# Low parts of the feed-forwards' own weight pool: subtracted on GpSimd instead of VectorE

## The chip, the cores and the metric

The kernel runs on one core of a Trainium2 chip. The metric is the device time of one execution in microseconds (us). The engines named below are TensorE (PE for its matmuls, PEld for its weight loads), VectorE (DVE), ScalarE (ACT), GpSimd (POOL) and SyncE (SP), whose queue issues the DMAs.

## The reference

256 tokens of 1024 features go through two transformer blocks, all in float32. What matters here is the feed-forward, which occurs six times with its own weights each time (two in the first block, four in the second):

```python
def swiglu(x, w_gate, w_up, w_down):      # [256,1024] x [1024,2816], [1024,2816], [2816,1024]
    return (jax.nn.silu(x @ w_gate) * (x @ w_up)) @ w_down

x = layer_norm(alpha * x + 0.5 * swiglu(x, ...))         # first block, twice, a hybrid attention mixer between them
h = h + 0.5 * _swiglu(_rmsnorm(h, g), w_gate_up, w_down)  # second block, four times, with a short
                                                          # convolution, shared keys and values, sparse attention between
```

## The kernel before

All weights arrive as float32 and are split into two parts of a type that TensorE takes at full rate: the high part is the rounded word (a copy on ScalarE), the low part is the word less its high part (a subtraction on VectorE). Every product is then three matmuls: high by high, high by low, low by high (`mm3`, lines 122 to 126). Activations are split in the same way after they were transposed on TensorE (`to_xt`, lines 232 to 246).

The function `unit` (lines 98 to 111) brings in a unit of weights, 128 partitions x 1024 words: one DMA of 512 KB on SP's queue into a tile `raw`, of which there are five; then, for each half of 512 columns, the copy on line 108 and the subtraction on line 109. A raw tile is free for a later DMA when both halves are subtracted. The parts go to tiles `whi` and `wlo`. By default these come from the pool `main`, six of each in a ring. With `pool=fp` they come from the pool of the feed-forward that is running, with the tag "d" and `nd` tiles of each (six; four in the fifth feed-forward). Two places ask for that:

```python
hi, lo = unit(wd[f * P:f * P + P, :], 1, D, fp, nd, "d")                      # line 418, down weights
sides.append(list(units(w, 0, 512, 2, **(dict(pool=fp, bufs=nd, tag="d") if i else {}))))   # line 384, first up weights
```

The pool `fp` is opened at the start of each `ffn` and takes the memory of the one before, so its tiles can be written when the feed-forward before has done with them.

A feed-forward goes as follows. `first` (lines 351 to 391) computes the first 512 hidden features token tile by token tile (two tiles of 128 tokens): gate and up for tile 0, then, after the transposes of tile 1, gate and up for tile 1. Its gate weights (four units) come from `main`; its up weights (four units) from `fp`, except in the very first feed-forward, where both come from `main`. For tile 0 the two transposes of tile 1's activations stand ahead of the last two of the eight chunks of the up product (`xt.ahead(1)`, line 388). Then `block` (lines 393 to 412) does 256 hidden features at a time with the weights stationary, nine times: gate (two units), up (two units), then the down product of the features before (`down`, lines 416 to 423: one unit for 128 features). The last six rows of down weights (four in the fifth) are kept and used at the end half by half, so that the residual, the norm and the transposes for what follows (`done`) can start while TensorE still works.

Between stages stands a chain through several engines: the residual add and the statistics on VectorE and ScalarE, the inverse root on GpSimd (`rsqrt`, line 230: a power on a column of 128 x 1), the scaling by the gains on VectorE (lines 278, 279, 303), the transposes on TensorE (line 238), their split by ScalarE and VectorE (lines 240, 241).

The order of the instructions on each engine's queue is set before the run by a planner that follows the program's order as priorities and its own estimate of when data and tiles are there; each engine then works its queue strictly in order and waits at its head. Only the instructions of the very first gate weights are kept in the program's order (`order=tc.keep_in_program_order`).

The five feed-forwards with first up weights in `fp` are called F2 to F6 below, in order of time. F2 follows the mixer's output projection, F3 follows F2 directly, F4 follows the convolution, F5 the shared keys and values, F6 the sparse attention's output projection.

Of the kernel before, what the change touches and what calls it, by code (L numbers as in the profile page):

```python
# [10 lines left out]
F32 = mybir.dt.float32  # L11
# [3 lines left out]
OP = mybir.AluOpType  # L15
# [19 lines left out]
def bcast_rows(ap, n, parts=P):  # L35
    """A DRAM vector of n elements, read into every partition."""
    return bass.AP(tensor=ap.tensor, offset=ap.offset, ap=[[0, parts], [1, n]])


class Turned(list):  # L40
    """Split transposes of activations; `need` brings in those of a tile of tokens, `ahead` a part of them."""

# [19 lines left out]
def weave(steps, others, rate):  # L62
    """After each of `steps`, `rate` of `others`."""
    due = 0.0
    for _ in steps:
        due += rate
        while due >= 1:
            next(others, None)
            due -= 1
# [3 lines left out]
def hybrid_blocks(  # L73
# [6 lines left out]
    nc = tc.nc  # L80
# [15 lines left out]

    # ---- weights: float32 words split into two float32r parts whose sum is exact
    def unit(src, nk, n, pool=None, bufs=6, tag="", order=lambda i: i):
        """src: DRAM [nk * 128, n] -> (high, low), each [128, nk, n]."""
        w = nk * n  # L100
        pool = pool or main
        raw = main.tile([P, UNIT], F32, tag="raw", name="raw", bufs=5)
        hi = pool.tile([P, UNIT], F32R, tag=f"whi{tag}", name="whi", bufs=bufs)
        lo = pool.tile([P, UNIT], F32R, tag=f"wlo{tag}", name="wlo", bufs=bufs)
        nc.sync.dma_start(raw[:, :w].rearrange("p (k n) -> p k n", k=nk),
                          src.rearrange("(k p) n -> p k n", p=P))
        for c in (slice(0, w // 2), slice(w // 2, w)):
            order(nc.scalar.activation(hi[:, c], raw[:, c], AF.Copy))  # L108
            order(nc.vector.tensor_tensor(lo[:, c], raw[:, c], hi[:, c].bitcast(F32), op=OP.subtract))  # L109
        return (hi[:, :w].rearrange("p (k n) -> p k n", k=nk),  # L110
                lo[:, :w].rearrange("p (k n) -> p k n", k=nk))

    def units(src, n0, n, per, **kw):
        """Columns n0:n0+n of src [K, N], `per` chunks of 128 rows at a time."""
        nk = src.shape[0] // P
        for k0 in range(0, nk, per):
            c = min(per, nk - k0)
# [4 lines left out]
    def mm3(ps, s, m, start, stop, **kw):  # L122
        """ps (+)= s.T @ m for split operands; what is dropped is the product of the low parts."""
        nc.tensor.matmul(ps, lhsT=s[0], rhs=m[0], start=start, stop=False, **kw)  # L124
# [3 lines left out]
    def projecting(xt, src, n0, n, done, per=2, lead=0, ws=None):  # L128
        """done(t, ps): ps[:, :n] = tokens of tile t @ src[:, n0:n0+n]; in steps. The first `lead` chunks go
        through one tile of tokens before they go through the other."""  # L130
        nk = src.shape[0] // P
# [35 lines left out]
    def projecting_t(xt, src, n0, nm, done, per=2):  # L167
        """done(m, ps): ps [128 features, 256 tokens] of feature tile m, from the column n0 on; in steps."""
        nk = src.shape[0] // P
# [21 lines left out]
    def projecting_wide(xt, src, done, nxt=None, at=1, tail=4, bank=None, k0=0):  # L191
        """done(t, h, ps): half h of tokens @ src [K, 1024]; the last rows tile by tile and half by half; in
        steps. nxt: what `done` goes on to turn."""
        nk = src.shape[0] // P
# [27 lines left out]

    # ---- constants
    ident = const.tile([P, P], F32)
# [7 lines left out]
    def to_xt(src, t, xt, nk=KD, k1=0, then=None):  # L232
        """Token-major src [128, nk * 128] -> split transposes in xt[:][:, k1:k1+nk, tile t]."""
        def turn(k0):
# [51 lines left out]
    def rms_stat(t, i):  # L286
        """Sum of the squares of half i; with the second one, the factors of the tile."""
        if i == 0:
# [42 lines left out]

    # ---- feed-forward
    def ffn(xt, wg, wu, wd, done, nxt=None, at=1, nd=6, tail=6, hook=None, ws=None):
        """Hidden features in blocks: the first token by token, so that it starts with one tile of
        tokens; the others with the weights stationary. Each block goes on into the down product."""
        with tc.tile_pool(name="ffn", bufs=1) as fp:
# [106 lines left out]

    # ======== first block
    xt = new_xt()
    ws = units(ffn_w_gate[0, 0], 0, 512, 1, order=tc.keep_in_program_order)
    head = []
# [18 lines left out]
    def later(**aps):  # L466
        """Gains that are read in the middle of the feed-forward."""
        def load(f0):
# [6 lines left out]

    # ---- mixer
    xt2 = new_xt()
    with tc.tile_pool(name="mix", bufs=1) as mp:
        win = w_in[0]
        def qkv(i, first, got):  # L480
            """Queries and keys [384 features, 256 tokens], values [tokens, 6, 64 and a one]."""
            c0 = 1152 * i
# [27 lines left out]
        def scores(qh, kh, slope, sums=None):  # L510
            """exp of the biased scores less their maximum; columns 0:128 for tile 0, the rest tile 1."""
            ps = tpb("s")
# [19 lines left out]
        def values(pt, ops, j, v, hh, w):  # L532
            """ops[:, t, j] = the turned weights of tile t @ v."""
            for b, t, kt in ((0, 0, 0), (1, 1, 0), (2, 1, 1)):
# [12 lines left out]
        def heads(weigh, v, w, end):  # L547
            """weigh(hh) gives the weights of a head; end(ops, h0) takes three heads @ values. In steps,
            each head's products one head behind its scores."""
            s, ops = {}, None  # L550
# [22 lines left out]
        def attend_diff(o, q, k, v):  # L573
            """Weights less lambda times the other ones, both over the sum of the first ones; the latter
            is divided by at the end."""
            r0 = mp.tile([P, NT, 6], F32, name="r0")
# [29 lines left out]
        def attend_sb(o, q, k, v):  # L606
            """Keys on partitions: columns 0:256 are keys of tile 0 with all queries, 256:384 keys of
            tile 1 with queries of tile 1. Two heads at a time, in steps."""
            nb = 2
# [55 lines left out]
        def gates(i, gt):  # L665
            """sigmoid(x) = (tanh(x / 2) + 1) / 2, of branch i."""
            for hf in range(2):
# [89 lines left out]
        def attend(i, steps, rest, rate):  # L757
            """The attention of branch i, with `rest` between its steps; its result is turned later."""
            o = o_tile()
# [25 lines left out]

    # ---- second feed-forward, into the second block
    xt1 = new_xt()
# [11 lines left out]

    # ======== second block  # L800
    def gate_up(l, i):
# [6 lines left out]

    # ---- short convolution, feature-major
    yt = new_xt()  # L810
# [65 lines left out]

    # ---- shared keys and values
    kv_stack = ctx.enter_context(ExitStack())
# [51 lines left out]

    # ---- compressed keys and values: blocks of 32 tokens as 16 chunks of two tokens
    posr = cmpp.tile([36, P], F32, name="posr")
# [7 lines left out]
    fs = new_xt()  # L940
    # for keys and for values: of 16 chunks the high parts of 64 blocks, then their low parts
    fs = [x.rearrange("p a b -> p (a b)").rearrange("p (j e n) -> p j e n", j=16, e=2) for x in fs]
# [93 lines left out]

    # ---- sparse attention: with 256 tokens all four blocks are selected and the window spans all
    with tc.tile_pool(name="nsa", bufs=1) as ap:
# [19 lines left out]

        # queries, high part on partitions 0:64 and low part on 64:128, head by head
        qs = new_xt()  # L1060
# [60 lines left out]

        # keys: window tile 1, window tile 0, compressed, selection tile 0, selection tile 1
        ks = tuple(ap.tile([P, 4, 528], F32R, name=f"ks{i}") for i in range(2))
        nc.scalar.activation(ks[0], kraw, AF.Copy)
        nc.vector.tensor_tensor(ks[1], kraw, ks[0].bitcast(F32), op=OP.subtract)

        # gates: high and low parts of their 48 columns of weights side by side
        graw = main.tile([P, UNIT], F32, tag="raw", name="graw", bufs=5)[:, 0:KD * 48].rearrange("p (k n) -> p k n", n=48)
# [20 lines left out]

        # compressed values, one diagonal block for each of 8 heads  # L1150
        vcb = ap.tile([P, 2, 8, HD], F32, name="vcb")
# [17 lines left out]
        def score(hh):  # L1169
            """Scores of one head against all its keys, and their exponentials."""  # L1170
            hf, hq, g = hh // 8, hh % 8, hh // 4
# [20 lines left out]
        def turn(hh):  # L1192
            """Keys onto partitions."""
            for b, s in enumerate(state[hh]):
# [25 lines left out]
        def compressed(hf):  # L1220
            """Weights of the compressed keys for eight heads, then their share of the output."""
            p3 = pc[hf].rearrange("p t h n -> p (t h) n")
# [117 lines left out]
```

## Time and profile before

| | |
|---|---|
| median of 3 runs | 1636.39 us (1635.88 to 1636.52) |
| span of the profiled execution | 1633.7 us |
| TensorE matmuls busy | 1617.4 us, 99% |
| TensorE weight loads busy | 1469.7 us, 90% |
| VectorE busy | 1035.8 us, 63% |
| ScalarE busy | 843.9 us, 52% |
| GpSimd busy | 51.1 us, 3% |
| 16 DMA engines | 56.9% on the weights' queue |
| TensorE's granted clock | full in all slices |

The profile gives no other time of the profiled execution than its span, from the first instruction to the last; the medians of the runs lie 2.7 us above it. Busy shares are means over stages. A wait is idle time of an engine and the event that ended it. Lines are those of the code before the change.

### The profile page before, as it was taken

How to read it: one execution, taken by the hardware profiler on the slowest of the kernel's cores; microseconds unless marked ns; L12 is line 12 of the kernel's file. 1: busy time of each engine (PE TensorE's matmuls, PEld its weight loads, DVE VectorE, ACT ScalarE, POOL GpSimd, SP SyncE). 2: the span in 40 equal slices, each digit the busy share in tenths (PEclk: the TensorE clock that was granted, in tenths of full speed). 3: DMA queues.
4: the chain of work that ended last, by engine and by line, in shares of the span. 5: the costliest groups of instructions: out<-in, count | busy, mean ns of one | idle time of the engine just before them, and what ended most of it. 6: DMA issues, size and time to landing. Idle time of an engine off the chain costs nothing.

```text
span 1633.7 us, 27122 instructions
## 1 busy us (share of the span) xinstructions
PE 1617.4 (99%) x10487; PEld 1469.7 (90%) x10487; DVE 1035.8 (63%) x2038; ACT 843.9 (52%) x1628; POOL 51.1 (3%) x101
## 2 busy tenths in 40 slices
PE   8999999999999999999999999999999999999999
PEld 7999899888799998999899899988899988889998
DVE  6655567768865458555566755557676568775552
ACT  6544266664564445444354644436546448664441
POOL 1000000000000000000000000001000012100000
PEclk9999999999999999999999999999999999999999
DMA  9756354555585666655455765646648522175550
GB/s 318 241 181 197 112 164 127 175 169 176 175 265 180 193 193 207 193 181 194 131 180 167 250 189 181 202 139 206 196 146 290 182 85 89 53 229 183 183 191 27
DMA packets 190222, 291.74 MB, mean 179 GB/s; under 512 B 11088, under 2 KB 135308, under 8 KB 190092
## 3 DMA queue, kind: packets, MB, share of 16 engines
q1 hardware_dynamic: 190092, 290.00, 56.9%
q8 instruction: 82, 1.34, 0.4%
q14 instruction: 48, 0.39, 0.1%
HBM read 288.91 MB, written 1.05 MB: 177 GB/s over the span
## 4 chain that ended last, share of the span: by engine, by line
PE 95%; DVE 2%; ACT 1%; DMA 1%; issue 1%; POOL 0%; SPq 0%; ACTq 0%; POOLq 0%
PE acc L124 21%; PE acc L126 21%; PE acc L125 21%; PE tp L124 8%; PE tp L125 8%; PE tp L126 8%; PE tp L238 1%; PE ops L1207 1%; PE tp L1197 1%; DVE wlo L109 1%; DMA raw<-in_ffn_w_gate_up_dram 1%; PE s L514 0%; PE acc L980 0%; PE ops L535 0%; ACT whi L108 0%
## 5 line engine op out<-in xcount | busy, mean ns | idle before, releaser
L109 DVE TENSOR_TENSOR wlo<-raw,whi 128x512 fp32r<-128x512 f32 (+2 forms) x1090 | 689.3, 674 | 412.8 <-ACT whi L108 409.8
L108 ACT ACTIVATE whi<-raw 128x512 fp32r<-128x512 f32 (+2 forms) x1090 | 615.0, 613 | 598.4 <-issue 324.7
L124 PE MATMUL acc<-xt,whi 128*128 128x256 f32 x2032 | 578.1, 285 | 0.0
L125 PE MATMUL acc<-xt,whi 128*128 128x256 f32 x2032 | 575.0, 283 | 0.0
L126 PE MATMUL acc<-xt,wlo 128*128 128x256 f32 x2032 | 574.1, 283 | 0.0
L124 PEld LDWEIGHTS acc<-xt,whi 128*128 128x128 f32 x2032 | 389.6, 192 | 3.2 <-ACT cg L823 0.2
L125 PEld LDWEIGHTS acc<-xt,whi 128*128 128x128 f32 x2032 | 389.7, 192 | 1.9
L126 PEld LDWEIGHTS acc<-xt,wlo 128*128 128x128 f32 x2032 | 389.3, 192 | 0.0
L124 PE MATMUL tp<-whi,hh 128*128 128x512 f32 x528 | 206.9, 392 | 0.0
L125 PE MATMUL tp<-wlo,hh 128*128 128x512 f32 x528 | 206.0, 390 | 0.0
L126 PE MATMUL tp<-whi,hh 128*128 128x512 f32 x528 | 205.6, 389 | 0.0
L124 PE MATMUL acc<-whi,xt 128*128 128x512 f32 (+1 forms) x448 | 178.2, 398 | 2.5 <-ACT xt L240 2.5
L126 PE MATMUL acc<-whi,xt 128*128 128x512 f32 (+1 forms) x448 | 174.2, 389 | 0.3 <-DVE xt L241 0.3
L125 PE MATMUL acc<-wlo,xt 128*128 128x512 f32 (+1 forms) x448 | 174.0, 388 | 0.0
L126 PEld LDWEIGHTS tp<-whi,hh 128*128 128x128 f32 x528 | 99.1, 188 | 21.0
L124 PEld LDWEIGHTS tp<-whi,hh 128*128 128x128 f32 x528 | 99.3, 188 | 19.2 <-ACT hh L411 0.3
L125 PEld LDWEIGHTS tp<-wlo,hh 128*128 128x128 f32 x528 | 99.3, 188 | 18.5
L124 PEld LDWEIGHTS acc<-whi,xt 128*128 128x128 f32 x448 | 84.6, 189 | 19.3 <-ACT xt L240 4.3
L126 PEld LDWEIGHTS acc<-whi,xt 128*128 128x128 f32 x448 | 84.4, 188 | 17.6 <-DVE xt L241 2.3
L125 PEld LDWEIGHTS acc<-wlo,xt 128*128 128x128 f32 x448 | 84.6, 189 | 14.6 <-DVE wlo L109 0.4
L409 DVE TENSOR_TENSOR hb<-acc,sg 128x512 f32<-128x512 f32 x54 | 37.3, 691 | 61.4 <-PE acc L126 61.3
L240 ACT ACTIVATE xt<-tp 128x512 fp32r<-128x512 f32 x48 | 28.1, 594 | 45.3 <-PE tp L238 45.0
(286 smaller groups left out, 1205.3 us busy)
## 6 DMA issues: line engine op xcount, KB each, us to landing
raw<-in_ffn_w_gate_up_dram SPq DMA_DIRECT2D x176, 512.0 KB, 4.5
raw<-in_ffn_w_down_dram SPq DMA_DIRECT2D x132, 512.0 KB, 3.8
raw<-in_ffn_w_up_dram SPq DMA_DIRECT2D x44, 512.0 KB, 5.0
raw<-in_ffn_w_gate_dram SPq DMA_DIRECT2D x40, 512.0 KB, 4.8
raw<-in_w_in_dram SPq DMA_DIRECT2D x36, 384.0 KB, 3.4
raw<-in_w_in_dram SPq DMA_DIRECT2D x24, 512.0 KB, 4.0
raw<-in_conv_w_in_dram SPq DMA_DIRECT2D x24, 512.0 KB, 4.4
raw<-in_kv_w_dram SPq DMA_DIRECT2D x12, 512.0 KB, 4.2
```

The costliest lines, as they stand in the source:

```text
L108: order(nc.scalar.activation(hi[:, c], raw[:, c], AF.Copy))
L109: order(nc.vector.tensor_tensor(lo[:, c], raw[:, c], hi[:, c].bitcast(F32), op=OP.subtract))
L124: nc.tensor.matmul(ps, lhsT=s[0], rhs=m[0], start=start, stop=False, **kw)
L125: nc.tensor.matmul(ps, lhsT=s[0], rhs=m[1], start=False, stop=False, **kw)
L126: nc.tensor.matmul(ps, lhsT=s[1], rhs=m[0], start=False, stop=stop, **kw)
L238: nc.tensor.transpose(tp[:, j, :], src[:, (k0 + j) * P:(k0 + j + 1) * P], ident)
L240: nc.scalar.activation(o[0], tp, AF.Copy)
L409: nc.vector.tensor_mul(hb, u, sg)
L1197: nc.tensor.transpose(tp[:, j * P:j * P + P], s[:, j * P:j * P + P], ident)
L1207: nc.tensor.matmul(ops[:, t, b, :], lhsT=pt[:, j * P:j * P + P], rhs=vs[:, b, kt, g, :], start=b == 0 and j == 0, stop=j != 1, skip_group_ ...
```

## The change

In `unit`, the engine of the subtraction now depends on the pool: units in `main` stay on VectorE, units in another pool are subtracted on GpSimd. Only the feed-forwards' pool is passed as another pool, so the down weights of all six feed-forwards and the first up weights of F2 to F6 move. The copies on ScalarE, the DMAs, the tiles and the matmuls are the same in number and shape. The planner orders the whole program anew. The rest of the diff takes out comments and docstrings.

```diff
         for c in (slice(0, w // 2), slice(w // 2, w)):
             order(nc.scalar.activation(hi[:, c], raw[:, c], AF.Copy))
-            order(nc.vector.tensor_tensor(lo[:, c], raw[:, c], hi[:, c].bitcast(F32), op=OP.subtract))
+            eng = nc.vector if pool is main else nc.gpsimd
+            order(eng.tensor_tensor(lo[:, c], raw[:, c], hi[:, c].bitcast(F32), op=OP.subtract))
```

## Rows read from the trace of the kernel before

**Rows 1.** The page, part 1: engine, busy us, share of the span, instructions.

```profile
PE 1617.4 (99%) x10487; PEld 1469.7 (90%) x10487; DVE 1035.8 (63%) x2038; ACT 843.9 (52%) x1628; POOL 51.1 (3%) x101
```

**Rows 2.** TensorE's waits, whole span: line and tile, releaser, total us, times, longest.

```profile
PE tp L238 <- DMA h<-in_x_dram: 5.1, 2, 4.1
PE acc L124 <- ACT xt L240: 2.5, 2, 1.9
...
PE tp L238 <- DVE xn L303: 0.8, 2, 0.6
```

**Rows 3.** One block of F2 by windows: length, PE, PEld, DVE, ACT, POOL busy.

```profile
537.79:554.77 16.98, 16.98 (x122) 16.02 (x121) 8.96 (x15) 7.70 (x15) 0.00 (x0) 1.00 0.62 186
```

**Rows 4.** Groups by line and form, VectorE: count, busy us, mean ns, idle before.

```profile
L109 DVE TENSOR_TENSOR wlo<-raw,whi 128x512 fp32r<-128x512 f32 x1002 | 645.7, 686 | 388.0 <-ACT whi L108 385.0 <-PE acc L126 0.4
```

**Rows 5.** Groups by line and form, GpSimd.

```profile
L453 POOL TENSOR_SCALAR h<-h 128x512 f32<-128x512 f32 x4 | 6.0, 1511 | 6.9 <-PE tp L238 6.9
...
L709 POOL TENSOR_SCALAR_AFFINE_SELECT ne<-ne 128x256 f32<-128x256 f32 x1 | 0.4, 402 | 0.0
...
L714 POOL TENSOR_SCALAR_AFFINE_SELECT negu<-negu 128x128 f32<-128x128 f32 x1 | 0.3, 296 | 0.0
```

**Rows 6.** Timeline, GpSimd and VectorE side by side: start, duration in us.

```profile
5.08 0.43 DVE L109 TENSOR_TENSOR wlo<-raw,whi 128x256 fp32r<-128x256 f32 x1 [4.13 <-ACT whi L108]
5.31 1.56 POOL L453 TENSOR_SCALAR h<-h 128x512 f32<-128x512 f32 x1 [3.93 <-PE tp L238]
5.42 0.83 DVE L109 TENSOR_TENSOR wlo<-raw,whi 128x256 fp32r<-128x256 f32 x1
...
1368.35 0.68 DVE L109 TENSOR_TENSOR wlo<-raw,whi 128x512 fp32r<-128x512 f32 x1
1368.51 0.70 POOL L1218 TENSOR_TENSOR on<-ob 128x64 f32<-128x64 f32 x1 [2.60 <-DVE ob L1214]
...
1378.30 0.32 POOL L1218 TENSOR_TENSOR on<-ob 128x64 f32<-128x64 f32 x1 [0.95 <-DVE ob L1214]
```

**Rows 7.** Timeline at F3's start, ScalarE, GpSimd, TensorE.

```profile
622.48 0.63 ACT L108 ACTIVATE whi<-raw 128x512 fp32r<-128x512 f32 x1
626.40 0.92 POOL L230 TENSOR_TENSOR st<-st,mhalf 128x1 f32<-128x1 f32 x1 [6.20 <-DVE st L273]
631.88 0.39 PE L125 MATMUL acc<-wlo,xt 128*128 128x512 f32 x1
632.69 0.65 PE L238 MATMUL tp<-ident,xn 128*128 128x128 f32 x4 [0.20 <-DVE xn L303]
633.95 0.50 PE L125 MATMUL acc<-wlo,xt 128*128 128x512 f32 x1
634.75 0.40 PE L125 MATMUL acc<-wlo,xt 128*128 128x512 f32 x1
```

**Rows 8.** Timeline at F4's start, ScalarE and TensorE.

```profile
906.77 0.62 ACT L108 ACTIVATE whi<-raw 128x512 fp32r<-128x512 f32 x1
918.94 0.40 PE L125 MATMUL acc<-wlo,xt 128*128 128x512 f32 x1
```

**Rows 9.** Timeline at F6's start, GpSimd, VectorE, TensorE.

```profile
1437.34 0.56 POOL L230 TENSOR_TENSOR st<-st,mhalf 128x1 f32<-128x1 f32 x1 [13.35 <-DVE st L296]
1437.90 0.69 DVE L109 TENSOR_TENSOR wlo<-raw,whi 128x512 fp32r<-128x512 f32 x1 [0.64 <-ACT whi L108]
1439.31 0.66 PE L238 MATMUL tp<-ident,xn 128*128 128x128 f32 x4
```

**Rows 10.** Timeline at the starts of F2 (two rows) and F5 (two rows).

```profile
438.16 1.15 ACT L108 ACTIVATE whi<-raw 128x512 fp32r<-128x512 f32 x2 [1.12 <-DMA raw<-in_ffn_w_up_dram]
445.64 0.40 PE L125 MATMUL acc<-wlo,xt 128*128 128x512 f32 x1
...
1128.50 2.71 ACT L108 ACTIVATE whi<-raw 128x512 fp32r<-128x512 f32 x5
1143.89 0.40 PE L125 MATMUL acc<-wlo,xt 128*128 128x512 f32 x1
```

## Prediction

> **What bounds the kernel now.** I read the busy times first. TensorE is busy in 99% of the span, VectorE in 63%, GpSimd in 3% [rows 1]. A busy TensorE may still be one that creeps, so I looked at one block of a feed-forward: 96 matmuls on 256 columns, 24 on 512. TensorE has no gap in its 16.98 us, while VectorE works 8.96 and ScalarE 7.70 [rows 3]. A stage with so much room on the other engines isn't waiting for VectorE. The third view is TensorE's waits. It lists nine kinds, 12.0 us in all, and the longest, 5.1 us, is the input's DMA at the start; behind it stands 2.5 us for a ScalarE split. None is a wait for a low part, and waits for VectorE's norm make 0.8 us [rows 2]. So little can be won, and the question is whether the new place can make TensorE wait.
>
> **What leaves VectorE.** 132 down units (22 in each of six feed-forwards) and 20 first up units (four in F2 to F6) have two halves each: 304 of the 1090 subtractions, all of 128x512. One costs VectorE 645.7 / 1002 = 0.64 us [rows 4], so 196 us go from its 1036. None of that was in TensorE's way, except where a subtraction stands in VectorE's queue ahead of a norm (F3, F6 below).
>
> **What one costs on GpSimd.** The trace has no subtraction of this shape there. From below: its one-input selections on 256 and 128 columns take 402 and 296 ns [rows 5], so 0.83 ns a column and 0.19 us fixed; 512 columns would be 0.61 us. From above: its two-input add on 64 columns takes 0.32 us undisturbed [rows 6]; eight of them are 2.56 us. Between: that add less the same fixed 0.19 is 2.0 ns a column, 1.23 us for 512; a one-tensor scaling of 128x512 takes 1.51 us [rows 5]. I take 1.3 us, near the only row with two tensor operands and somewhat towards the one of the right size. 304 of them are 395 us, a quarter of the span, where 51 are busy now.
>
> The Trainium skill (GPSIMD Engine Reference, Elementwise — side-by-side cycle accounting) gives 4497 ns for a two-input add on 2048 float32 columns. A quarter, as an estimate, is 1.12 us; by it F3 and F4 below would come out in time, and the change would cost about 0.5 us.
>
> **Steady blocks: nothing.** A block of 16.98 us brings four moved subtractions, 5.2 us of GpSimd's time, and leaves VectorE some 6.4 of its 8.96. The down weights have a ring of three blocks' length, and TensorE doesn't wait for their low parts although they pass the same five raw tiles as everything else. A raw tile comes free up to 2 x (1.3 - 0.64) = 1.3 us later, so SP's queue, which stands in order behind it, issues the next weights that much later; they are wanted a block later. If this cover were gone, 1.3 us in each of 54 blocks would be 70 us. I count 0, for ends of 0 and that.
>
> **The starts of F2 to F6.** Here eight up subtractions have to be made in a row while TensorE eats one half every 0.68 us (three matmuls of 0.227), and they share GpSimd's queue with the inverse roots. I compare the time at which GpSimd would be done with the time at which TensorE now takes the low part.
>
> *F3* follows F2 directly, so its tiles come free only when F2's last matmuls end: the first up copy starts at 622.48 and is done at 623.11 [rows 7]. Behind it, in GpSimd's queue, come the subtractions and both roots of tile 1 (0.92 us each beside VectorE [rows 7], say 1.8). The sixth is done at 623.11 + 6 x 1.3 + 1.8 = 632.7, and its matmul now starts at 631.88: 0.8 late. The eighth is done at 635.3, against 634.75, inside that delay. On the other side VectorE has lost eight subtractions between the steps of tile 1's norm, so the 0.20 us for which TensorE waits at 632.69 go. What is late next is the low part, not the norm. With 0.4 for meetings at the port (next but one paragraph): 0.8 - 0.2 + 0.4 = 1.0 us.
>
> *F4*: the first copy is done at 907.39, eight subtractions and one root of 0.9 end at 918.7, and the last low part is taken at 918.94 [rows 8]. In time by 0.25; with 0.4 at the port, 0.2 us late.
>
> *F6*: the root of tile 0 runs at 1437.34, and the transposes that need it start at 1439.31 [rows 9], practically without slack. It can now stand behind one subtraction, up to 1.3 us. But the VectorE subtraction of 0.69 at 1437.90 [rows 9], which stood ahead of the scaling, is gone. 1.3 - 0.6 at worst, below nothing at best; I take 0.3.
>
> *F2* and *F5*: in F2 the last up copy ends at 439.31; four subtractions after it end at 444.5, and TensorE takes the last at 445.64. In F5 the copies start at 1128.50, eight subtractions end at 1139.5, the last is taken at 1143.89 [rows 10]. Both 0. The first feed-forward has no first up weights in the pool: 0.
>
> **Meetings at the port.** A VectorE subtraction of 256 columns that began beside GpSimd's 1.56 us scaling took 0.83 instead of 0.43 us, and a GpSimd add that began in a VectorE subtraction took 0.70 instead of 0.32 [rows 6]. So each kind holds up the other by about 0.4 us. In F3 and F4 one such hold-up is counted, since the rest falls into gaps; six (one for each scaling of tile 1) would be 2.3.
>
> The Trainium skill says it more sharply (SBUF — State Buffer, Who interferes with whom): VectorE with two SBUF inputs and a GpSimd instruction that reads SBUF exclude each other for the whole instruction. The rows agree that they interfere; that VectorE's instruction ended at 6.25, before GpSimd's at 6.87, does not fit a lock of whole length.
>
> **The sum**: 1.0 + 0.2 + 0.3 = 1.5 us. On the span of 1633.7 that is 1635.2; the runs' median lies 2.7 us above the span, which the change doesn't touch, so 1637.9 us. 0.2%, what a measurement of this kernel can tell from no change, is 3.3 us: 1633.1 to 1639.7 counts as no change.
>
> **Rivals.**
> 1. *GpSimd is the bound at the starts* (slower). Every 0.1 us more than 1.3 adds 0.8 us in F3 and 0.8 in F4, since eight stand in a row. At 1.6: F3 3.4 - 0.2 = 3.2, F4 2.5, F6 0.6, F2 0.1, sum 6.4, 1642.8 us. At the upper end of 2.56: F3 11, F4 10, F5 5.7, F2 3.9, about 32, 1668 us. It decides from 1.41 us, where the sum passes 3.3. For it: the scaling of 1.51 us. Against: the add's 1.23.
> 2. *Whole instructions exclude each other* (slower): the skill's rule above. VectorE's six scalings of 0.7 us in F3 then stand between GpSimd's subtractions (4.2 instead of 0.4, +3.8), as do two scalings and four subtractions in F4 (+3.8), and the two scalings on F6's path each wait up to 1.3 (+2). 1.5 + 9.6 = 11, 1647.5 us. Against: the 0.40 beside 1.56 us [rows 6].
> 3. *The relief is worth something* (faster). If the low parts are in time and the planner's new order also spares waits, the 0.8 us for the norm [rows 2] go: 1635.6. To pass 0.2% it would also need the 2.5 us that ScalarE's splits cost [rows 2], 1633.1, and nothing in the change shortens ScalarE's queue.
>
> **Chances**: forecast with its neighbours inside the bound 0.55, the first rival 0.30, the second 0.09, the third, beyond 0.2%, 0.06. So faster 0.06, same 0.55, slower 0.39. The range goes from 1634.8 (low parts in time, norm waits gone, a little more) to 1645.5, the first rival at about 1.75 us; the rest of the first rival, half of the second and the third stay outside. Inside the likeliest case it is 1635.5 to 1639.7.
>
> **What would show it.** GpSimd's group of subtractions: 304 with a mean near 1.3 us, longer beside VectorE; VectorE busy near 840 us. TensorE's waits: new ones, on the low part from GpSimd, at the starts of F3 and F4 alone, about a microsecond each; blocks still 16.98 us. Wrong would be: a mean above 1.4, waits for low parts in the blocks or in F2 and F5, a root that waits longer than one subtraction, or a wait for raw tiles that reaches TensorE.

## The result, and the profile after

1660.05 us (median; 1657.73 to 1661.52) against 1636.20: ratio 1.0145, interval 1.0131 to 1.0160. The change costs 23.8 us. The forecast was 1637.9 in a range of 1634.8 to 1645.5, so it was wrong. The profiled execution has a span of 1656.0 us, 22.3 more than before. In the code after the change, lines behind 109 stand one lower: the subtraction is L110, the transposes L239, the RMS scaling L304, the layer norm's L279 and L280, the root L231.

Page, part 1, after:

```profile
PE 1625.0 (98%) x10487; PEld 1472.2 (89%) x10487; DVE 977.4 (59%) x1734; ACT 842.1 (51%) x1628; POOL 481.7 (29%) x405
```

TensorE has the same 10487 matmuls as in [rows 1]. Its idle time went from 1633.7 - 1617.4 = 16.3 to 1656.0 - 1625.0 = 31.0 us (+14.7), and its busy time rose by 7.6 us: together the 22.3. VectorE lost 304 instructions, 196 us by [rows 4], but its busy time fell by only 58. Something made the remaining ones longer. First the moved group as part 5 of the page has it, then groups of VectorE by line and form, after and before (count, busy us, mean ns, idle before):

```profile
L110 POOL TENSOR_TENSOR wlo<-raw,whi 128x512 fp32r<-128x512 f32 x304 | 431.6, 1444 | 727.0 <-ACT whi L108 609.8
```

```profile
L110 DVE TENSOR_TENSOR wlo<-raw,whi 128x512 fp32r<-128x512 f32 x698 | 566.7, 846 | 431.8 <-ACT whi L108 430.1
...
L304 DVE SCALAR_TENSOR_TENSOR xn<-h,st,gain 128x512 f32<-128x512 f32 x28 | 26.0, 964 | 9.7 <-POOL st L231 9.7
...
L280 DVE SCALAR_TENSOR_TENSOR h<-xn,st,gain 128x512 f32<-128x512 f32 x12 | 12.5, 1085 | 1.7 <-POOL st L231 1.7
```

```profile
L303 DVE SCALAR_TENSOR_TENSOR xn<-h,st,gain 128x512 f32<-128x512 f32 x28 | 19.9, 748 | 6.8 <-POOL st L230 6.8
...
L279 DVE SCALAR_TENSOR_TENSOR h<-xn,st,gain 128x512 f32<-128x512 f32 x12 | 8.4, 745 | 0.0
```

GpSimd's subtraction takes 1.44 us in the mean (minimum 1.26, median 1.30). VectorE's own subtraction of the same form grew from 686 ns [rows 4] to 846. The norms' scalings went from 748 (RMS) and 745 (layer norm) to 964 and 1085.

TensorE's waits after, and its busy time in stretches of 4 us: at the starts of F2 and F3 after, then one at F2's start before (columns: length, busy with count, granted clock, DMA share, GB/s):

```profile
PE tp L239 <- DVE xn L304: 7.2, 4, 4.5
...
PE acc L125 <- ACT xt L241: 4.3, 3, 2.5
PE acc L127 <- DVE xt L242: 2.5, 4, 1.0
...
PE acc L126 <- POOL wlo L110: 0.7, 1, 0.7
```

```profile
432.00:436.00 4.00, 1.20 (x4) 0.92 0.58 181
436.00:440.00 4.00, 3.95 (x9) 0.50 0.59 213
440.00:444.00 4.00, 4.00 (x14) 0.73 0.87 256
...
636.00:640.00 4.00, 2.29 (x9) 1.00 0.54 160
640.00:644.00 4.00, 0.52 (x3) 0.52 0.60 223
644.00:648.00 4.00, 4.00 (x16) 0.63 0.80 263
```

```profile
432.00:436.00 4.00, 2.10 (x10) 1.00 0.66 182
```

The low parts from GpSimd make TensorE wait 0.7 us, the scalings 7.2 (0.8 before [rows 2]), the splits of the activations, `xt`, 6.8 (2.8 before). At both starts TensorE idles about 3 and 5 us, and then works at 0.50 of full clock, the 1.2 GHz level, for a few microseconds. That is most of the 7.6 us by which its busy time rose: the mean granted clock of the span is 0.996, which over 1656 us is 6 to 7 us.

Where the loss sits shows at one landmark of each feed-forward, the first transpose of its first hidden features. Before, then after, for F2 to F6 (start, duration):

```profile
462.76 0.27 PE L366 MATMUL tp<-ident,hb 128*128 128x128 f32 x1
651.85 0.27 PE L366 MATMUL tp<-ident,hb 128*128 128x128 f32 x1
936.06 0.27 PE L366 MATMUL tp<-ident,hb 128*128 128x128 f32 x1
1161.18 0.27 PE L366 MATMUL tp<-ident,hb 128*128 128x128 f32 x1
1471.00 0.27 PE L366 MATMUL tp<-ident,hb 128*128 128x128 f32 x1
```

```profile
467.49 0.27 PE L367 MATMUL tp<-ident,hb 128*128 128x128 f32 x1
664.08 0.27 PE L367 MATMUL tp<-ident,hb 128*128 128x128 f32 x1
950.64 0.27 PE L367 MATMUL tp<-ident,hb 128*128 128x128 f32 x1
1179.68 0.27 PE L367 MATMUL tp<-ident,hb 128*128 128x128 f32 x1
1493.31 0.27 PE L367 MATMUL tp<-ident,hb 128*128 128x128 f32 x1
```

The lag is 4.7, 12.2, 14.6, 18.5, 22.3 us. So the starts of F2 and F3 cost 4.7 and 7.5 us, the stretch to F4's landmark 2.4, F4's first block and F5's start 3.9, and F6's start 3.8. From there to the end, nothing. The steady blocks are as before; one of F2 (columns as in [rows 3]):

```profile
542.52:559.50 16.98, 16.98 (x123) 16.02 (x122) 8.33 (x10) 7.70 (x16) 5.76 (x4) 1.00 0.57 183
```

GpSimd works 5.76 us in it, and TensorE still has no gap in 16.98 us.

What happens at a start is plainest at F6, in the timeline of GpSimd and VectorE:

```profile
1457.92 0.56 POOL L231 TENSOR_TENSOR st<-st,mhalf 128x1 f32<-128x1 f32 x1
1458.45 1.26 POOL L110 TENSOR_TENSOR wlo<-raw,whi 128x512 fp32r<-128x512 f32 x1
1458.51 1.74 DVE L304 SCALAR_TENSOR_TENSOR xn<-h,st,gain 128x512 f32<-128x512 f32 x1 [1.79 <-POOL st L231]
1459.67 1.72 POOL L110 TENSOR_TENSOR wlo<-raw,whi 128x512 fp32r<-128x512 f32 x1
1460.18 1.76 DVE L304 SCALAR_TENSOR_TENSOR xn<-h,st,gain 128x512 f32<-128x512 f32 x1
```

The scaling that begins just behind GpSimd's subtraction takes 1.74 us instead of 0.75. GpSimd's next one, behind that scaling, takes 1.72, and the second scaling 1.76. They take turns, and TensorE waits for both scalings.

At F3, the start with the largest loss, the root is late as well (statistic and scalings on VectorE, root on GpSimd; x2 is a row of two):

```profile
630.83 0.15 DVE L274 TENSOR_SCALAR st<-mv 128x1 f32<-128x1 f32 x1
630.90 2.72 DVE L279 SCALAR_TENSOR_TENSOR xn<-h,mv,gain 128x512 f32<-128x512 f32 x2
634.74 0.54 POOL L231 TENSOR_TENSOR st<-st,mhalf 128x1 f32<-128x1 f32 x1
635.31 3.46 DVE L280 SCALAR_TENSOR_TENSOR h<-xn,st,gain 128x512 f32<-128x512 f32 x2 [1.69 <-POOL st L231]
...
641.67 3.43 DVE L304 SCALAR_TENSOR_TENSOR xn<-h,st,gain 128x512 f32<-128x512 f32 x2 [1.75 <-POOL st L231]
```

The root stands 3.8 us behind a running subtraction and two more, and VectorE loses 1.69 us by it. The six scalings of tile 1 take 9.6 us together; before, they took 4.2.

### The profile page after: what moved, and what is told of

It reads as the page before. It is cut to its first block, busy times and chain, and to the rows that moved or that the text cites. A ratio compares the mean times of both kernels' runs of the same rounds, so it can differ in the third digit from the quotient of the medians.

```text
span 1656.0 us, 27188 instructions
## 1 busy us (share of the span) xinstructions
PE 1625.0 (98%) x10487; PEld 1472.2 (89%) x10487; DVE 977.4 (59%) x1734; ACT 842.1 (51%) x1628; POOL 481.7 (29%) x405
## 4 chain that ended last, share of the span: by engine, by line
PE 90%; DVE 3%; DMA 2%; ACT 2%; issue 1%; POOL 1%; SPq 0%; ACTq 0%; POOLq 0%
PE acc L125 20%; PE acc L127 20%; PE acc L126 20%; PE tp L125 8%; PE tp L127 8%; PE tp L126 8%; DMA raw<-in_ffn_w_gate_up_dram 1%; POOL wlo L110 1%; ACT whi L108 1%; PE tp L239 1%; PE ops L1208 1%; DVE wlo L110 1%; PE tp L1198 1%; PE s L515 0%; PE acc L981 0%
## 5 line engine op out<-in xcount | busy, mean ns | idle before, releaser
L110 DVE TENSOR_TENSOR wlo<-raw,whi 128x512 fp32r<-128x512 f32 (+2 forms) x786 | 610.4, 811 | 454.0 <-ACT whi L108 452.2
L110 POOL TENSOR_TENSOR wlo<-raw,whi 128x512 fp32r<-128x512 f32 x304 | 431.6, 1444 | 727.0 <-ACT whi L108 609.8
L125 PE MATMUL acc<-whi,xt 128*128 128x512 f32 (+1 forms) x448 | 180.2, 402 | 4.4 <-ACT xt L241 4.3
L127 PE MATMUL acc<-whi,xt 128*128 128x512 f32 (+1 forms) x448 | 176.1, 393 | 2.6 <-DVE xt L242 2.5
```

What stands on the lines that cost most here:

```text
L110: order(eng.tensor_tensor(lo[:, c], raw[:, c], hi[:, c].bitcast(F32), op=OP.subtract))
L127: nc.tensor.matmul(ps, lhsT=s[1], rhs=m[0], start=False, stop=stop, **kw)
```

## The experiments

Theories when the runs began: the lock (rival 2: an instruction on VectorE with two tensors in SBUF and one on GpSimd exclude each other); the queue (the roots stand behind GpSimd's subtractions); the order (the planner's new order costs the time); a slow GpSimd (rival 1). A fourth came from the traces: the raw tile (GpSimd holds it longer, so SP loads later, and ScalarE's queue stands at a copy with other work behind it). Medians of the kernel before lay between 1635.99 and 1637.0 beside these experiments, and each ratio is to the kernel before of the same series.

**E1, the lock by itself.** A program of its own: rows of the same instruction on VectorE, on GpSimd, and on both at once.

> A program of its own, none of the blocks' work: eight GpSimd subtractions of 128x512 (two float32 operands in SBUF, output as the low parts have it) beside sixteen VectorE instructions, and each kind alone. Alone: VectorE subtraction 0.62 us from one to the next, GpSimd 1.26 (the shortest in the changed kernel). Lock theory (a GpSimd instruction and a VectorE one with two SBUF operands exclude each other for nearly their whole length): together VectorE's take up to 1.7 us and the stretch about 16 x 0.62 + 8 x 1.26 = 20 us instead of 10; with one operand in PSUM, and beside a memset, no such lengthening. Sharing theory (each costs the other some 0.4 us, as forecast): VectorE's 1.0 us, the stretch about 13 us.

Timeline, VectorE, then GpSimd (start, duration of the row of 8 or 16; tile `ps` is in PSUM). VectorE's first row is alone; its rows of 16 stand beside eight of GpSimd's: four beside the subtraction, the one at 120.17 beside the one-tensor scaling, the last beside a memset:

```profile
2.68 5.78 DVE L98 TENSOR_TENSOR dv<-a,b 128x512 fp32r<-128x512 f32 x8
...
53.57 19.12 DVE L98 TENSOR_TENSOR dv<-a,b 128x512 fp32r<-128x512 f32 x16 [28.48 <-SPq L122]
72.82 19.82 DVE L101 SCALAR_TENSOR_TENSOR dv<-a,s,b 128x512 f32<-128x512 f32 x16
92.77 11.57 DVE L104 TENSOR_TENSOR dv<-ps,b 128x512 fp32r<-128x512 f32 x16
104.47 15.57 DVE L107 TENSOR_SCALAR dv<-a,s 128x512 f32<-128x512 f32 x16
120.17 13.88 DVE L98 TENSOR_TENSOR dv<-a,b 128x512 fp32r<-128x512 f32 x16
134.54 11.59 DVE L98 TENSOR_TENSOR dv<-a,b 128x512 fp32r<-128x512 f32 x16 [0.48 <-SPq L122]
```

```profile
25.29 10.64 POOL L110 TENSOR_TENSOR po<-a,b 128x512 fp32r<-128x512 f32 x8 [24.85 <-SPq L122]
...
53.62 13.44 POOL L110 TENSOR_TENSOR po<-a,b 128x512 fp32r<-128x512 f32 x8 [0.20 <-SPq L122]
...
92.81 10.69 POOL L110 TENSOR_TENSOR po<-a,b 128x512 fp32r<-128x512 f32 x8 [7.01 <-SPq L122]
```

Alone, 16 subtractions on VectorE are 11.6 us (twice the 5.78 of eight). Beside eight of GpSimd's they are 19.1: 7.6 us more, about 0.95 for each of GpSimd's eight, which take 1.33 each alone (10.64) and lose 0.35 each (13.44). With one operand in PSUM nothing is lost on either side. Beside GpSimd's one-tensor scaling the loss is only 2.3 us. (VectorE's own one-tensor scaling is held too: 15.6 us for 16 beside GpSimd's subtraction, where eight alone took 4.14.) So GpSimd's two-tensor subtraction locks out VectorE's SBUF work, and its one-tensor scaling hardly does. The pair on which the prediction rested [rows 6] was the mild one.

**E2 and E3, one half of the change each.**

```diff
# in `unit`, not shown: low.tensor_tensor(...) with low=nc.vector by default
-    hi, lo = unit(wd[f * P:f * P + P, :], 1, D, fp, nd, "d")
+    hi, lo = unit(wd[f * P:f * P + P, :], 1, D, fp, nd, "d", low=nc.gpsimd)      # E2: down weights
-    ... dict(pool=fp, bufs=nd, tag="d") ...
+    ... dict(pool=fp, bufs=nd, tag="d", low=nc.gpsimd) ...                        # E3: first up weights
```

> Only the 264 subtractions of the down weights on GpSimd; the 40 of the first up weights stay on VectorE. SP's queue then has the order of the kernel before, so this also takes away the new DMA order. Theory of the starts (what costs is GpSimd's work beside VectorE's norms and subtractions and in front of the roots while a feed-forward starts): within 3 us of the kernel before, 1634 to 1639 us. Theory of the whole (GpSimd as a slow worker on all moved weights, raw tiles given back late in every block): 264 of 304 of the loss stays, about 1657 us.

> Only the 40 subtractions of the first up weights on GpSimd, the down weights back on VectorE. SP's queue has the order of the changed kernel. Theory of the starts: 1653 to 1660 us, nearly all of the loss with 40 of 304 subtractions. Theory of the whole: 40 of 304 of the loss, about 1640 us.

E2: 1643.23, ratio 1.0039 (1.0024 to 1.0054). E3: 1655.47, 1.0118 (1.0101 to 1.0135). Alone, the 40 up subtractions cost 19.2 us and the 264 others 6.9, together a little more than the 23.8 of both at once. E2 lies above the range that the theory of the starts gave it.

**E4, roots on VectorE.** In the changed kernel the root becomes a minimum with a constant on VectorE (the root itself is left out).

> The changed kernel, but the inverse roots are replaced by a minimum with a constant on VectorE (the power is left out), so that no norm waits in GpSimd's queue behind subtractions. Lock theory: VectorE's scalings still stand beside GpSimd's subtractions and take 1.7 us, so most stays: 1650 to 1657 us. Queue theory (the roots behind up to two subtractions of 1.26 us are what costs): the starts of F3 and F6 lose their waits and F3 its stretch of lower clock, 1640 to 1646 us.

1658.8, 1.0139 (1.0124 to 1.0154): not to be told from the change. The loss doesn't need the queued roots.

**E5, one tensor on GpSimd.** Every engine keeps the changed kernel's order.

```diff
# moved units only, shortened
-  eng.tensor_tensor(lo[:, c], raw[:, c], hi[:, c].bitcast(F32), op=OP.subtract)
+  nc.gpsimd.tensor_scalar(lo[:, c], hi[:, c].bitcast(F32), raw[:, c.start:c.start + 1], None, op0=OP.mult)
```

> All 304 moved instructions stay on GpSimd, in the place and with the waits of the changed kernel, but each multiplies the high part by one column of the raw tile (one tensor operand; what it leaves out: the low parts of these weights, which then hold another number) instead of subtracting two tensors. Every engine's order is that of the changed kernel, the instruction is longer (about 1.5 us instead of 1.3). Theory of the lock (VectorE stands still during a GpSimd instruction with two tensor operands): VectorE's scalings come back from 1.75 to about 0.75 us and the time to 1637 to 1643, with a waiting time of TensorE for the scalings under 2 us. Theory of the order (the planner's other order of instructions and weight loads costs the time): nothing changes, 1655 to 1660. Theory of a slow GpSimd (its instruction's own length makes low parts late): longer instructions, so slower than the changed kernel, 1660 to 1667, with TensorE waiting for low parts.

1665.79, 1.0178: the lock theory's forecast failed outright, and the slow GpSimd's came in. GpSimd's instruction now takes 1.69 us. The RMS scalings by line and form:

```profile
L303 DVE SCALAR_TENSOR_TENSOR xn<-h,st,gain 128x512 f32<-128x512 f32 x28 | 21.2, 793 | 14.2 <-POOL st L230 14.2
```

The scalings did come back (793 ns, from 964), but VectorE now waits 14.2 us for the roots behind GpSimd's longer instructions (9.7 in the changed kernel, 6.8 before), and the norm is late again. With several ways of being late, taking one away shows little.

**E6, the steady blocks alone** (`low=nc.gpsimd if 4 <= f < FC - tail else nc.vector` for the down weights).

> Only the down weights of the steady blocks (hidden chunks 4 up to those taken last) are subtracted on GpSimd; the first four chunks and the late ones stay on VectorE. Theory of the lock, paid where TensorE has nothing ready to do (the norms and splits at the ends and starts of the feed-forwards): 1636 to 1638.5, no wait over 0.5 us in the blocks. Rival: the steady blocks themselves pay (a split of the hidden features held up in many blocks a little): 1640 to 1644, as with all down weights moved, and TensorE's waits for hidden features stay.

1637.91, ratio 1.0007 (0.9998 to 1.0017): no price that can be told from none.

**E7, a memset in the place of the subtraction** (`nc.gpsimd.memset(lo[:, c].bitcast(F32), 0.0)`, moved units only).

> Each of the 304 moved subtractions is replaced by a memset of the same low-part tile on GpSimd (what it leaves out: the low parts of these weights are zero). TensorE's order is exactly the changed kernel's, other engines' nearly. GpSimd then works some 0.6 us an instruction, waits for no copy, holds no raw tile and, by the measured pairs, holds up no VectorE instruction; what stays of the change is the order and the 304 subtractions that VectorE no longer makes. Theory of the order: it stays near the changed kernel, above 1650. Theories that put the loss into GpSimd's instructions (lock, roots queued behind them, raw tiles held, low parts late): 1634 to 1638, as before the change; if the relief of VectorE is worth anything, it shows here as a time below 1634.

1633.64, 0.998 (0.997 to 0.999). TensorE's order is the changed kernel's, so its order is not the cause; SP's, VectorE's and ScalarE's differ from it in the place of a few instructions. The kernel is even 2.7 us faster than before. In that lie the relief of VectorE, raw tiles that come free earlier (the memset reads none) and the new order; no run parts the three.

**E8 to E12 and E15 to E17: the ways of being late, in combination.** "Raw free" reads the high part only, so the raw tile is free once ScalarE has copied it. "Two" subtracts two tensors, "one" multiplies one tensor by a column. E9 and E11 subtract the high part from itself, E16 the raw tile from itself; E15 and E17 subtract a constant tile (the identity) from the high part.

> The one-tensor multiplication of e5 in place of the subtraction (the low parts of these weights hold another number), and the inverse roots as a minimum with a constant on VectorE as in e4 (the root itself left out); each engine's order is that of e4. Theory that lock and queue both cause the loss, each enough by itself to make the norm late: with both gone 1639 to 1648 (GpSimd's instruction is 0.4 us longer, so low parts may come late at the starts). Theory of the lock alone: no better than e5, 1660 to 1667, since e5 had taken it away already. Theory of raw tiles held by GpSimd (SP's queue issues the next weights late, ScalarE's queue stands at a weight copy with a split of activations behind it): 1655 to 1667, since the longer instruction holds them longer.

> The moved subtraction reads the high part twice instead of the raw tile and the high part (what it leaves out: the low parts of these weights are zero); still two tensors in SBUF, still 1.3 us, in GpSimd's queue at the same place, so lock and queued roots stay. Only the raw tile comes free as soon as ScalarE has copied it. Theory of the raw tiles: most of the loss goes, 1637 to 1645. Theories of lock and queue: it stays, 1653 to 1662.

> As e9, order and all, but with one tensor operand: the high part times one of its own columns (the low parts hold another number). What is taken away beside e5 is the hold on the raw tile alone; beside e9 the second tensor, and the instruction grows from 1.15 to some 1.7 us. Theory of the raw tiles: well below e5's 1665.8, by 10 us or more. Of what e9 keeps (1647.3 against 1633.6 of the memset): if it is the lock, 1636 to 1643 here; if it is the time that GpSimd takes (roots queued, low parts late), it grows with the instruction, 1648 to 1656.

> As e9 (two tensors, both the high part; the low parts are zero), with the inverse roots as a minimum on VectorE (the root left out), so neither raw tile nor queued root is left, only the lock and a little lateness. If e9's remaining loss is the lock on VectorE's own instructions: it stays, 1643 to 1648. If it is the roots queued behind the subtractions: 1635 to 1641.

> One tensor operand, the high part alone, and the roots on VectorE (the low parts hold another number, the root is left out): no lock, no raw tile, no queued root; left are 304 instructions of some 1.7 us, whose low parts come late where eight stand in a row. If the three reasons together are the whole: 1636 to 1642, TensorE waiting for low parts in two or three places. If the length of the instruction alone costs: above 1648.

> As e9, in exactly its order, but the moved instruction subtracts a constant tile (the 128-column identity, repeated) from the high part, so it has two different tensors in SBUF again and its length should be that of the changed kernel's (the low parts hold another number). The raw tile is free as soon as ScalarE has copied it. Theory of the raw tiles: 1646 to 1651. Rival (e9 gained by its shorter instruction): 1654 to 1662.

> The moved instruction subtracts the raw tile from itself (the low parts are zero): the short form of e9, and SP's order is e9's, but the raw tile is held until GpSimd is done with it; it no longer waits for ScalarE's copy. Theory of the raw tiles: 1652 to 1660, near the changed kernel. Rival (the hold doesn't matter; order or length did it): 1645 to 1649, as e9.

> As e15 (constant tile subtracted from the high part, two different tensors, raw tile free at once), with the inverse roots as a minimum on VectorE (the root left out), in e11's order: of the three reasons only the lock is left. Theory that the lock alone is most of it: 1650 to 1656, against 1637.2 of e12, which differs in the second operand only and whose instruction is longer. Rival (roots and raw tiles are the larger part): 1638 to 1645.

| GpSimd's instruction, mean us | raw held, roots on GpSimd | raw held, roots on VectorE | raw free, roots on GpSimd | raw free, roots on VectorE |
|---|---|---|---|---|
| two tensors, 1.44 | the change 1660.05 | E4 1658.80 | E15 1655.82 | E17 1654.65 |
| one tensor, 1.64 to 1.71 | E5 1665.79 | E8 1658.37 | E10 1649.50 | E12 1637.19 |
| same tensor twice, 1.15 to 1.16 | E16 1648.59 | | E9 1647.31 | E11 1643.45 |

The kernels of one column share one order on TensorE, VectorE, ScalarE and SP, save E16, whose SP order is that of the raw-free columns; E7 has the order of the third column. Between raw held and raw free the order differs in the place of a few instructions (on SP, of three loads of gains for the norms); TensorE's is the same. E8 to E10 came out near what the raw theory expected (E9 2.3 us above its range), E15 and E16 in its rival's ranges, E11 and E17 in the lock theory's, E12 where it should lie if the three reasons are the whole. Three readings:

- *The lock alone is enough.* E17 and E12 differ in the moved instruction alone (a second tensor against one column), have neither a held raw tile nor a queued root, and E17's instruction is the shorter one: 1654.65 against 1637.19, 17.5 us, or 16.9 by the ratios to the kernel before (1.0107, 1.0090 to 1.0124, and 1.0004, 0.9994 to 1.0013). That is the lock's; about 5 us of it are the half clock that follows its waits (mean granted clock 0.997 in E17, 1.0 in E12). TensorE's waits in E17, then in E12, where the RMS scalings are not among them:

```profile
PE tp L238 <- DVE xn L303: 5.5, 3, 3.9
...
PE acc L125 <- DVE wlo L109: 4.7, 3, 3.2
```

```profile
PE acc L124 <- ACT xt L240: 1.5, 2, 1.3
...
PE acc L125 <- POOL wlo L109: 1.2, 2, 0.6
```

- *On top of the lock little is left to tell apart.* The held raw tile brings 4.2 us (the change against E15, E4 against E17; 3.3 and 5.2 by the ratios), and the intervals of each pair overlap or touch. The queued roots bring 1.2 us (E15 against E17, the change against E4), which is within the noise. Without the lock, but with an instruction of some 1.7 us, each is enough by itself: held raw tiles bring 21 us (E8 against E12), queued roots 12 (E10 against E12). So the ways overlap, and their shares can't be added up. What is called the raw tile's share includes the moved loads. SP's queue waits 417 us for GpSimd's instructions in E8 and not at all in E12, and 8.9 and 8.4 us for its gains, which speaks for the hold, but no run parts the two at full length. E9's 12.7 us against the change, which I first took for the raw tile, were mostly its shorter instruction: E15, with the full length, gives 8.5 of them back, and E16, which holds the tile with a short instruction, is only 1.3 slower than E9.
- *GpSimd's length as such is not the bound.* In E12 the instruction takes 1.65 us, and the low parts cost 1.2 us.

How a held raw tile reaches TensorE shows in F4's first block, in the changed kernel's timeline:

```profile
950.10 1.72 POOL L110 TENSOR_TENSOR wlo<-raw,whi 128x512 fp32r<-128x512 f32 x1
951.85 0.34 SPq L105 DMA_DIRECT2D raw<-in_ffn_w_down_dram  x1
955.45 0.63 ACT L108 ACTIVATE whi<-raw 128x512 fp32r<-128x512 f32 x1 [5.49 <-DMA raw<-in_ffn_w_down_dram]
958.46 0.37 ACT L370 ACTIVATE hh<-tp 128x256 fp32r<-128x256 f32 x1
958.87 0.42 DVE L371 TENSOR_TENSOR hh<-tp,hh 128x256 fp32r<-128x256 f32 x1 [5.29 <-ACT hh L370]
```

GpSimd's subtraction ends, itself stretched to 1.72; only then does SP issue the next load of down weights. ScalarE stands 5.49 us at its copy, the copy of the hidden features stands behind that, and TensorE waits 1.1 us for it.

**E13, four raw tiles in the kernel before**, nothing on GpSimd (`bufs=4` in place of 5).

> The kernel before the change, with four raw tiles in place of five; nothing is moved to GpSimd. Theory of the raw tiles (the weights' supply has little to spare at the starts of the feed-forwards, so a tile that is held a few us longer reaches TensorE): clearly slower, 1642 to 1660, with the lost time at the starts and TensorE waiting for splits that stand behind weight copies on ScalarE. Rival (five tiles are plenty, and the loss came from something else that reading the raw tile does, as meetings at the memory): 1635 to 1639.

1641.39, ratio 1.0028 (1.0017 to 1.0040), just under the lower end of the raw theory's range: the supply has little to spare, but a tile less costs 5 us, not 15. The planner's order is another too, so the size is rough.

**E14, raw tiles and a queue of their own for the moved weights**, with real subtractions.

```diff
# shortened
+  raw = main.tile(... bufs=4) if pool is main else pool.tile([P, UNIT], F32, tag="rawd", bufs=2 if bufs > 4 else 1)
-  nc.sync.dma_start(raw...)
+  (nc.sync if pool is main else nc.gpsimd).dma_start(raw...)
```

> The change, with real subtractions on GpSimd, but the moved weights have raw tiles of their own (two in F1 to F5, one in F6) which GpSimd's queue loads; the other weights keep four tiles on SP's queue. The lock and the queued roots stay. Theory of the raw tiles: SP's and ScalarE's queues no longer stand behind GpSimd's subtraction, so 1643 to 1651, like e9, or the time of e13 where four tiles are too few. Rival (issuing loads from GpSimd behind its own subtractions makes the moved weights late, and with two tiles more so): 1655 to 1680, TensorE waiting for low parts.

1725.71, 1.0555: worse than either side said. TensorE waits for weight copies (11.8 us in the largest group) and for GpSimd's low parts (6.5) all over. The kernel has four tiles for the rest, two for the moved (one in F5, where the text above says F6), another queue and another order at once, so it says nothing about the hold; it is no way out.

**E18, down weights from the fifth hidden chunk on** (`f >= 4`, the late ones too).

> Down weights from the fifth hidden chunk on, the late ones too, are subtracted on GpSimd; the first four chunks of each feed-forward stay on VectorE. If the loss of e2 (1643.2) sits at the first four chunks, where their copies stand in ScalarE's queue ahead of the first block's splits: 1636 to 1639. If it sits at the end of a feed-forward, where the late ones meet the norms: 1641 to 1645.

1638.78, 1.0010 (1.0001 to 1.0019). Of E2's 6.9 us over the kernel before, 1.8 are left. So about 5 come with the first four chunks of each feed-forward, which belong to its start too.

No version with the real subtraction beats the kernel before: E6 is level with it.

## Why the prediction was wrong

The failing step is "Meetings at the port". It took 0.4 us for a meeting, counted one each in F3 and F4 "since the rest falls into gaps", and put six meetings at 2.3 us. Measured: a VectorE instruction with two SBUF tensors that meets GpSimd's subtraction takes about 1.0 us more (1.74 for 0.75 at F6), and at a start they meet again and again, because GpSimd has eight in a row: F3's six scalings take 9.6 us for 4.2. E17 against E12 gives 17.5 us for what the step put at 0.8. The evidence was [rows 6], where GpSimd's instruction has one tensor. E1 shows that this pair costs 2.3 us where the real pair costs 7.6. A row of the right shape and engine, but with another number of operands, was no price for this one, and the only row with two tensors on GpSimd (0.70 for 0.32, on 64 columns) held less than a VectorE instruction's length.

Rival 2 had the mechanism, with a chance of 0.09 and 1647.5 us. The Trainium skill (SBUF — State Buffer, Who interferes with whom) says that VectorE with two SBUF inputs contends with a GpSimd instruction that reads SBUF, and that the second to come is blocked for the whole instruction. For two tensors on each side the runs agree nearly: 19.1 us for 11.6 in E1, which is 0.95 us of GpSimd's 1.33 a meeting. For GpSimd's one-tensor form they don't (13.9 for 11.6), which is why [rows 6] seemed to refute it. Rival 2's 11 us counted the direct hold-ups in F3, F4 and F6 only. It missed F2 (4.7 us), the half clock after TensorE's idle stretches in F2 and F3, and what held raw tiles and late roots add.

The other steps:

- *1.3 us for one subtraction*: median 1.30; the mean of 1.44, over the 1.4 that the prediction named as a sign of being wrong, comes with the meetings.
- *Steady blocks nothing*: right for 148 of the 264 down subtractions. A block is 16.98 us, and E6 has a ratio of 1.0007. But "steady" begins at the fifth chunk: the first four chunks of down weights are part of the start, and they cost about 5 us (E2 less E18). The prediction called the later release of raw tiles covered; F4's first block shows one that reaches TensorE. How much of the 5 us is the hold and how much the lock was not parted.
- *F3 1.0, F4 0.2, F6 0.3, F2 and F5 0*: measured 7.5 (F3), 2.4 and a part of 3.9 (F4; the rest is F5's), 3.8 (F6) and 4.7 (F2). The reckoning set GpSimd's finish against TensorE's need of the low part. For the low part that was nearly right: TensorE waits 0.7 us for one in F3, where 0.8 was predicted. But the low part was not what came last; the norm's scalings and the splits of activations were. "What is late next is the low part, not the norm" had it the wrong way round.
- *Rival 1* (GpSimd slow, low parts late): no. E12's instruction is longer than the 1.41 us from which the rival was to decide, and TensorE waits 1.2 us for its low parts in all; the ratio of 1.0004 can't be told from none. A longer instruction does cost where roots queue behind it or raw tiles are held (E10, E8).
- *Rival 3* (the relief): at most small. E7's 2.7 us contain it, with two other things, and nothing of it is seen beside the lock.
- *Root behind one subtraction*: true at F6, where the root starts 1.2 us after its statistic, but at F3 it waits 3.8 us, behind three. The prediction counted F3's roots as time of GpSimd's and not as a delay of the norm. Beside the lock this is worth 1.2 us (E4), within the noise.

Not settled: what a subtraction of 1.3 us without the lock would cost with held raw tiles and queued roots; the one-tensor form run here takes 1.56 us at the least. Nor is the held raw tile parted from the few moved loads. That half clock follows the idle stretches shows in the windows, but no run changed one and kept the other.

## What to carry to other kernels

Before work goes to GpSimd, list what VectorE runs in the same microseconds, and which of it TensorE waits for. If both sides read two tensors from SBUF they take turns: at F6 such a meeting cost VectorE about 1.0 us beside GpSimd's 1.3, and GpSimd 0.4 beside VectorE's 0.75. Work that fills a steady stage for nothing can be dear at a stage's start, so give it by stage, not by kind. And when several ways of being late overlap, one edit at a time shows little: E5 by itself would have cleared the lock, and E4 the roots. What showed the cause was to take all of them away (E12) and put one back (E17).

## What the runs showed of the hardware

- GpSimd on 128x512: subtraction of two tensors 1.30 us, of a tensor from itself 1.04, one-tensor scaling 1.56, memset 0.53. The one-tensor scaling is not cheaper than the two-tensor subtraction.
- VectorE beside GpSimd's two-tensor subtraction (E1, 16 instructions): two SBUF tensors 19.1 us, one SBUF tensor 15.6, one of two in PSUM 11.6. Alone, eight take 5.78, 4.14 and 5.77.
- TensorE at F2's start: busy 1.20 us from 432 to 436 us, then at the 1.2 GHz level (0.50); before the change it was busy 2.10 us in the same stretch, and the granted clock stayed at full.
